# A two-layer decoder trunk on one Trainium2 core: stick-breaking attention with queries on partitions, its suffix sums by a VectorE scan and its probabilities turned through DRAM

## The chip, the cores and the metric

The kernel runs on one core of one Trainium2 chip. The metric is the device time of one execution in microseconds (us), the median of several runs. Times of single instructions, waits and transfers come from the hardware profiler's record of one execution. The engines are named as in the profile: PE (TensorE, the matmuls) with PEld (its weight loads), DVE (VectorE), ACT (ScalarE), POOL (GpSimd) and SP (SyncE, which issues most of the weight transfers). "ACTq" and "SPq" are the queues on which ACT and SP issue DMAs.

## The reference

A residual stream of 272 tokens (16 learned meta tokens and 256 of the sequence) by 2048 goes through two layers. Each layer is a token mixer with 16 heads of 128 and a squared-ReLU MLP of 8192. Layer 0 mixes with a softmax attention that has a forget gate. Layer 1 mixes with stick-breaking attention, whose K and V come from one projection `w_kv`; it is the part that the change touches:

```python
def stick_breaking_attention(q, k, v):
    for qs, qe in query_blocks(q.shape[1]):          # 16, then 128, then 128 queries
        z = einsum('bqhd,bkhd->bhqk', q[:, qs:qe], k[:, :qe]) * scale
        mask = k_pos[None, :] < q_pos[:, None]
        log_beta = log_sigmoid(z)
        log_one_minus = where(mask, log_sigmoid(-z), 0.0)
        suffix = cumsum(log_one_minus, axis=3, reverse=True) - log_one_minus
        a = where(mask, exp(log_beta + suffix), 0.0)
        outs.append(einsum('bhqk,bkhd->bqhd', a, v[:, :qe]))
```

With e = softplus(z), the logarithm of a probability is z minus the sum of e over this key and all later keys that the query sees. So a sum that runs backwards over the keys is wanted for each query and head. Only the 256 sequence tokens leave the kernel (after a last norm), so layer 1 has 256 queries and 272 keys.

## The kernel before

**The weight matmuls.** Activations lie with features on partitions and tokens on the free axis. All projections go through `gemm_group` (line 230): 512 output features, as four accumulators of 128 (`pacc`, four PSUM buffers), over four k blocks of 512 input features, 48 matmuls a block. Full f32 precision is had from split operands: each weight tile `raw` is copied by ACT to a rounded `whi` (line 225), and VectorE makes the rest, `wlo = raw - whi` (line 226); three matmuls (hi by hi, hi by lo, lo by hi) stand for one (line 192). A k block has two weight halves, so two `whi` and two `wlo`. `raw`, `whi` and `wlo` have four buffers each, that is two k blocks' worth. SP loads `raw` (line 214). Blocks 0 and 3 of a group go accumulator by accumulator and so need both halves at once; blocks 1 and 2 take the first half, then the second. The next group's accumulator m waits for the evacuation of this group's accumulator m by VectorE (`evac_kv`, line 472).

**Order.** The matmuls of PE are pinned one behind another in the order in which they are written (`gemm_matmul`, line 190); `placed_behind` and `behind` pin other instructions behind given matmuls. The list `issued` holds the matmuls of the running group, so `issued[140]` is its 141st. On each engine the rest is ordered by a scheduler at build time; each engine then runs its instructions in that order, and so does each engine's DMA queue: an instruction that waits holds back everything behind it, on ACT also the DMAs that ACT issues.

**Layer 0's attention (lines 462 to 609).** It has queries on partitions: `ps` of 144 and 272 keys, a softmax along the free axis, and then the probabilities must be turned, since the product with V sums over keys on partitions. They are turned in two steps: VectorE transposes 32 x 32 squares (line 543) into a tile `raw_p`, four DMAs write it to a scratch `p_dram` (line 546) and two DMAs read it back with the squares put in their places (line 567); then ACT and VectorE split the part that needs it.

**Layer 1's attention (lines 688 to 809).** A loop over four groups g of four heads. Each turn runs a K group of `w_kv`, the scores and probabilities, and a V group of `w_kv`; the products with V are the function `outputs1`, called ahead of k block 3 of the next turn's K group (line 690), and behind the last V group for g = 3. Then `out_proj` follows.

- Scores have keys on partitions: `pza` (128 keys by 256 queries, three matmuls of split operands) and `pzb` (the second 128 keys by the 144 queries that see them). The last 16 keys ("corner") are packed for four heads into one tile `kc` by POOL and have scores of their own, 64 columns.
- `softplus` (lines 693 to 698): three ACT passes and one on VectorE give e. Then e is split into `eh` (line 748) and `el` (line 749).
- The backward sums are matmuls with constant triangles: `ntri_r` (minus one at and above) and `nones_r` (all minus one), lines 756 to 761, six per pair of heads, into `pta` and `ptb`; `corner_sums` (lines 706 to 712) does the same for the corner.
- VectorE adds the sums to the scores (lines 765 to 768), ACT takes the exponential (line 773), and the part of the first 128 keys is split. The probabilities have keys on partitions already, as the product with V wants them.
- V is turned to token-major, for g below 3, by the same means as layer 0's probabilities: `squares` (line 401), `scratch` with eight writes to `v_dram` (line 412) and `values_back` with two reads (line 419), all on ACT's queue. For g = 3 PE turns it (`token_major`, line 389).

The tag "pp" names three SBUF slots of 1024 f32 a partition that are handed around between `e`, `eh`, `el`, `turned` and others; a new tile of a tag waits until the oldest of the three is done with.

## Time and profile before

| what | value |
| --- | --- |
| median of 3 runs | 2281.2 us (2281.03 to 2281.36) |
| span of the profiled execution | 2278.5 us |
| PE busy | 2271.1 us, 18898 matmuls |
| DVE busy | 1333.5 us |
| ACT busy | 1065.1 us |
| POOL busy | 39.4 us |
| HBM read and written | 413.85 MB and 8.41 MB |

The span is from the first to the last instruction of one execution; the run's time has some 2.7 us around it. "Busy" sums the time in which an engine executes, without the time in which it waits. A timeline row shows the start, the duration, the engine, the source line, the operation, the output and inputs, the shapes and how many instructions the row holds; in square brackets stands how long the engine had been idle before it and which instruction ended that. Matmuls are pipelined, so their durations overlap: what one costs a full PE is the distance between starts. A row that groups instructions by line gives the total and, behind the comma, the mean in ns.

### The profile page before, as it was taken

The page shows a single profiled execution, that of the slowest core. Times are in us where ns is not written, and L with a number is a line of the kernel's source. Part 1 is how long each engine was busy: PE and PEld are TensorE (multiplying, and loading weights), DVE is VectorE, ACT ScalarE, POOL GpSimd, SP SyncE. Part 2 cuts the span into 40 slices and gives each one's busy share as a digit, 9 for nine tenths or more (in the row PEclk, how much of TensorE's full clock was granted, in tenths as well). Part 3 has the DMA queues.
Part 4 walks back from the last instruction along what each step waited for, and adds up shares of the span by engine and source line. Part 5 has one row for each costly group of instructions (what it writes and reads, how often), then busy time and mean ns, then how long its engine had stood idle before and what let it go on. Part 6 is the DMA issues. An engine that isn't in the chain of part 4 may idle for free.

```text
span 2278.5 us, 44956 instructions
## 1 busy us (share of the span) xinstructions
PE 2271.1 (100%) x18898; PEld 2262.8 (99%) x18898; DVE 1333.5 (59%) x1930; ACT 1065.1 (47%) x1471; POOL 39.4 (2%) x72
## 2 busy tenths in 40 slices
PE   9999999999999999999999999999999999999998
PEld 9999999999999999999999999999999999999998
DVE  7767566554455455455566666666555555555555
ACT  6444445443354344335445555555443544543554
POOL 1000000000000000000000000000000000000001
PEclk9999999999999999999999999999999999999999
DMA  7765665555555555555556555555656556566564
GB/s 238 228 198 188 222 184 176 181 172 180 182 176 185 167 185 179 174 185 169 186 183 193 168 174 169 167 185 190 202 187 201 192 189 201 184 200 195 186 201 141
DMA packets 146171, 425.19 MB, mean 187 GB/s; under 512 B 31648, under 2 KB 43824, under 8 KB 145968
## 3 DMA queue, kind: packets, MB, share of 16 engines
q1 hardware_dynamic: 113760, 406.29, 54.1%
q10 hardware_dynamic: 32208, 16.02, 2.6%
q8 instruction: 148, 2.42, 0.4%
q14 instruction: 55, 0.45, 0.1%
HBM read 413.85 MB, written 8.41 MB: 185 GB/s over the span
## 4 chain that ended last, share of the span: by engine, by line
PE 99%; DMA 0%; issue 0%; POOL 0%; SPq 0%; POOLq 0%; ACT 0%; DVE 0%
PE acc L192 97%; PE po L435 0%; PE ps L435 0%; PE pza L435 0%; DMA raw<-w_qkv 0%; PE pzb L735 0%; PE po L804 0%; PE ps L508 0%; PE po L603 0%; PE pf L354 0%; PE pta L757 0%; PE pta L756 0%; PE pv L394 0%; POOL ob L850 0%; PE ptb L709 0%
## 5 line engine op out<-in xcount | busy, mean ns | idle before, releaser
L226 DVE TENSOR_TENSOR wlo<-raw,whi 128x1024 fp32r<-128x1024 f32 (+1 forms) x773 | 928.5, 1216 | 715.6 <-ACT whi L225 706.6
L225 ACT ACTIVATE whi<-raw 128x1024 fp32r<-128x1024 f32 (+1 forms) x773 | 796.4, 1050 | 961.0 <-PE acc L192 913.4
L192 PE MATMUL acc<-x_m,whi 128*128 128x272 f32 (+1 forms) x4096 | 643.1, 282 | 0.0
L192 PE MATMUL acc<-x_u,whi 128*128 128x272 f32 (+1 forms) x3968 | 626.0, 282 | 0.0
L192 PEld LDWEIGHTS acc<-x_m,whi 128*128 128x128 f32 x4096 | 566.0, 188 | 0.1
L192 PEld LDWEIGHTS acc<-x_u,whi 128*128 128x128 f32 x3968 | 550.4, 188 | 0.0
L192 PE MATMUL acc<-x_m,wlo 128*128 128x272 f32 (+1 forms) x2048 | 441.4, 282 | 0.0
L192 PE MATMUL acc<-x_u,wlo 128*128 128x272 f32 (+1 forms) x1984 | 432.1, 282 | 0.0
L192 PE MATMUL acc<-x_a,whi 128*128 128x272 f32 (+1 forms) x2048 | 355.4, 286 | 0.2 <-ACT whi L225 0.2
L192 PEld LDWEIGHTS acc<-x_m,wlo 128*128 128x128 f32 x2048 | 323.5, 188 | 0.0
L192 PEld LDWEIGHTS acc<-x_u,wlo 128*128 128x128 f32 x1984 | 315.3, 188 | 0.0
L192 PEld LDWEIGHTS acc<-x_a,whi 128*128 128x128 f32 x2048 | 301.3, 189 | 1.7 <-ACT whi L225 1.1
L192 PE MATMUL acc<-x_a,wlo 128*128 128x272 f32 (+1 forms) x1024 | 253.8, 286 | 0.0
L192 PE MATMUL acc<-x_kv,whi 128*128 128x272 f32 x1024 | 191.7, 288 | 0.0
L192 PEld LDWEIGHTS acc<-x_a,wlo 128*128 128x128 f32 x1024 | 175.7, 188 | 0.7 <-DVE ssq_a L158 0.4
L192 PE MATMUL acc<-x_o,whi 128*128 128x272 f32 (+1 forms) x1024 | 163.1, 283 | 0.0
L192 PEld LDWEIGHTS acc<-x_kv,whi 128*128 128x128 f32 x1024 | 160.1, 189 | 0.1
L192 PE MATMUL acc<-x_kv,wlo 128*128 128x272 f32 x512 | 147.6, 288 | 0.0
L192 PEld LDWEIGHTS acc<-x_o,whi 128*128 128x128 f32 x1024 | 142.3, 188 | 0.0
L307 DVE TENSOR_TENSOR hT<-acc,hT 128x272 f32<-128x272 f32 (+1 forms) x156 | 67.3, 431 | 75.4 <-PE acc L192 75.2
L192 PE MATMUL acc<-x_o,wlo 128*128 128x272 f32 (+1 forms) x512 | 110.7, 282 | 0.0
L192 PEld LDWEIGHTS acc<-x_kv,wlo 128*128 128x128 f32 x512 | 96.6, 189 | 0.0
(255 smaller groups left out, 1065.5 us busy)
## 6 DMA issues: line engine op xcount, KB each, us to landing
raw<-w_up SPq DMA_DIRECT2D x256, 512.0 KB, 3.9
raw<-w_dn SPq DMA_DIRECT2D x256, 512.0 KB, 4.0
raw<-w_qkv SPq DMA_DIRECT2D x92, 512.0 KB, 4.3
raw<-w_o SPq DMA_DIRECT2D x64, 512.0 KB, 3.9
raw<-w_kv SPq DMA_DIRECT2D x64, 512.0 KB, 4.4
raw<-w_q SPq DMA_DIRECT2D x32, 512.0 KB, 4.7
p_dram<-raw_p ACTq DMA_DIRECT2D x32, 96.0 KB, 4.6
v_dram<-turned ACTq DMA_DIRECT2D x48, 64.0 KB, 3.8
```

Of the source, the lines that this page charges most:

```text
L192: ins = nc.tensor.matmul(*args, **kw).ins
L225: on_act = nc.scalar.activation(hp, src, AF.Copy)
L226: on_dve = nc.vector.tensor_tensor(out=lp, in0=src, in1=hp.bitcast(F32), op=ALU.subtract)
L307: nc.vector.tensor_tensor(out=hT[:, c, t0:], in0=acc, in1=hT[:, c, t0:], op=ALU.add)
```

## The change

Layer 1's scores, probabilities and corner blocks are computed as in layer 0, with queries on partitions, and the triangular matmuls go.

- The constants `ntri`, `nones` and their copies and `maskC` go; `maskB` becomes 416 wide for the two query blocks (144 and 272 keys); `goes_on` is new, ones with a zero at the first place of each of the four runs of keys.
- The scores of a head: queries 128 to 255 by 272 keys with split operands (q2 against k, whose low half lies in a spare part of the output tile), queries 0 to 127 by 144 keys in f32. One VectorE add of the mask per head.
- `softplus` on 832 elements, then one `tensor_tensor_scan` of VectorE per pair of heads: state = state x goes_on + e, with e read backwards, so each run of keys starts anew. The scores minus the sums, read backwards, go through exp.
- `turn_probabilities` and `probabilities_back` are layer 0's turn through `p_dram`, made functions and used by both layers: six VectorE transposes, four DMA writes and two DMA reads per pair. In layer 1 the reads are pinned behind matmuls 140 and 176 of the V group, and the splits behind its last matmul.
- The corner probabilities are packed by POOL, transposed by PE (`pm`) and multiplied with `maskD`, as in layer 0, and the output tail is 128 columns wide.

```diff
+    def turn_probabilities(s, raw, pr):
+        y = raw[:, :768].rearrange("p (c h b i) -> p c h b i", c=4, h=2, b=3)
+        for i in range(2):
+            for b, o in enumerate((0, 144, 144 + P)):
+                nc.vector.transpose(y[:, :, i, b, :], s[:, 2 * pr + i, o:o + P].rearrange("p (c k) -> p c k", c=4))
+        y = y.rearrange("p c h b i -> p c (h b i)")
+        for a in range(4):
+            nc.scalar.dma_start(p_dram[pr].rearrange("c j a x -> a j c x")[a], y[32 * a:32 * a + 32])
+
+    def probabilities_back(pps, places):
+        for pr, at in enumerate(places):
+            raw, p0, p1 = pps[pr]
+            back = p_dram[pr].rearrange("c j a (h x) -> (c j) (a h) x", h=2)
+            for dst, src in ((raw[:, :512], back[:, :, :64]), (p1.rearrange("p i q -> p (i q)"), back[:, :, 64:])):
+                behind(nc.scalar.dma_start(dst.rearrange("p (m x) -> p m x", m=8), src), issued[at])
...
+        k0 = att.tile([P, 4, T], F32R, tag="vT", bufs=1, name=f"k0_{g}")
+        k1 = ao.spare[:, 4 * g:4 * g + 4]
+        for j in range(0, 4, 2):
+            nc.scalar.activation(k0[:, j:j + 2], kT[:, j:j + 2], AF.Copy)
+            nc.vector.tensor_tensor(out=k1[:, j:j + 2], in0=kT[:, j:j + 2], in1=k0[:, j:j + 2].bitcast(F32),
+                                    op=ALU.subtract)
+        q2 = att.tile([P, 2, 4, P], F32R, tag="pp", bufs=3, name=f"q12_{g}")
+        split(q2, q[:, :, P:S])
...
         for pr in range(2):
-            nc.tensor.matmul(pa, ntri_r, e_hi[:, :, 0:256], start=True, stop=False)
-            nc.tensor.matmul(pa, ntri_r, e_lo[:, :, 0:256], start=False, stop=False)
-            nc.tensor.matmul(pa[:, :, 112:], nones_r, e_hi[:, :, 256:400], start=False, stop=False)
-            nc.tensor.matmul(pa[:, :, 112:], nones_r, e_lo[:, :, 256:400], start=False, stop=True)
-            nc.tensor.matmul(pb[:, :, :144], ntri_r, e_hi[:, :, 256:400], start=True, stop=False)
-            product = nc.tensor.matmul(pb[:, :, :144], ntri_r, e_lo[:, :, 256:400], start=False, stop=True)
...
+            zp = z[:, 2 * pr:2 * pr + 2]
             for i in range(2):
+                product = by_parts(ps[:, 144:416], [q2[:, k, j, :] for k in range(2)], [k0[:, j], k1[:, j]], True, True)
+                placed_behind(nc.tensor.matmul(ps[:, 0:144], q[:, j, 0:P], kT[:, j, :144], start=True, stop=True), product)
+                nc.vector.tensor_tensor(out=z[:, j], in0=ps[:, :416], in1=maskB, op=ALU.add)
+            softplus(e.rearrange("p (i k) -> p i k", i=2), zp)
+            nc.vector.tensor_tensor_scan(out=sums, data0=goes_on.rearrange("p i k -> p (i k)"), data1=backward(e), initial=0.0,
+                                         op0=ALU.mult, op1=ALU.add)
+            nc.vector.tensor_tensor(out=zf, in0=zf, in1=backward(sums), op=ALU.subtract)
+            nc.scalar.activation(zp, zp, AF.Exp)
+            raw = att.tile([P, 2, 2, 256], F32, tag="pp", bufs=3, name=f"raw_p1_{g}_{pr}").rearrange("p x i q -> p (x i q)")
...
+            turn_probabilities(z, raw, pr)
+            pps.append((raw, p0, p1))
...
         gemm_group(w_kv[2 * g + 1], xc, 0, lambda m, acc: evac_kv(m, acc, vT))
+        probabilities_back(pps, (140, 176))
+        for pr in range(2):
+            raw, p0, p1 = pps[pr]
+            behind(split(p0.rearrange("p x i q -> p x (i q)"), raw[:, :512]), issued[-1])
```

In the order that each engine gets at build time, SP's list of instructions is the same before and after; ACT's queue has 22 transfers instead of 10 in each of the groups 0 to 2.

More of the change, by code (lines that the diff above doesn't have):

```diff
@@ L63, in yoco_kernel @@
     make_identity(nc, ident)
-    nones = const.tile([P, P], F32, name="nones")
-    nc.vector.memset(nones, -1.0)
-    nones_r = const.tile([P, P], F32R, name="nones_r")
-    nc.vector.tensor_copy(nones_r, nones)
-    ntri = const.tile([P, P], F32, name="ntri")
-    nc.gpsimd.memset(ntri, -1.0)
-    nc.gpsimd.affine_select(out=ntri, in_=ntri, compare_op=ALU.is_ge, fill=0.0, base=0,
-                            pattern=[[-1, P]], channel_multiplier=1)
-    ntri_r = const.tile([P, P], F32R, name="ntri_r")
-    nc.vector.tensor_copy(ntri_r, ntri)
     maskA = const.tile([P, 416], F32, name="maskA")
@@ L89, in yoco_kernel @@
                             pattern=[[32, 4], [0, 32]], channel_multiplier=-1)
-    maskB = const.tile([P, 400], F32, name="maskB")
+    maskB = const.tile([P, 416], F32, name="maskB")
     nc.gpsimd.memset(maskB, 0.0)
-    nc.gpsimd.affine_select(out=maskB[:, 0:256], in_=maskB[:, 0:256], compare_op=ALU.is_gt, fill=-BIG,
-                            base=M, pattern=[[1, 256]], channel_multiplier=-1)
-    nc.gpsimd.affine_select(out=maskB[:, 256:400], in_=maskB[:, 256:400], compare_op=ALU.is_gt, fill=-BIG,
-                            base=0, pattern=[[1, 144]], channel_multiplier=-1)
-    maskC = const.tile([P, 4, M], F32, name="maskC")
-    nc.gpsimd.memset(maskC, 0.0)
-    nc.gpsimd.affine_select(out=maskC, in_=maskC, compare_op=ALU.is_gt, fill=-BIG, base=M,
-                            pattern=[[32, 4], [1, M]], channel_multiplier=-1)
-    nc.gpsimd.affine_select(out=maskC, in_=maskC, compare_op=ALU.is_ge, fill=-BIG, base=-M,
-                            pattern=[[-32, 4], [0, M]], channel_multiplier=1)
+    nc.gpsimd.affine_select(out=maskB[:, 0:144], in_=maskB[:, 0:144], compare_op=ALU.is_gt, fill=-BIG,
+                            base=M, pattern=[[-1, 144]], channel_multiplier=1)
+    nc.gpsimd.affine_select(out=maskB[:, 144:416], in_=maskB[:, 144:416], compare_op=ALU.is_gt, fill=-BIG,
+                            base=M + P, pattern=[[-1, T]], channel_multiplier=1)
+    goes_on = const.tile([P, 2, 416], F32, name="goes_on")
+    nc.gpsimd.memset(goes_on, 1.0)
+    for t in (0, T):
+        nc.gpsimd.memset(goes_on[:, :, t:t + 1], 0.0)
     maskD = const.tile([P, 8, M], F32, name="maskD")
@@ L132, in __init__ @@
             if t0:
-                self.wide = rows[:, :, :n + 6]
+                self.wide, self.spare = rows[:, :, :n + 6], rows[:, :, d:d + T]
                 nc.gpsimd.tensor_copy(rows[:, :, n:n + 6], pad[:, :6].unsqueeze(1).to_broadcast([P, NC, 6]))
@@ L459, in put_split, with in_order @@
         nc.vector.tensor_tensor(out=lo, in0=src, in1=hi.bitcast(F32), op=ALU.subtract)
+    def turn_probabilities(s, raw, pr):
[12 more added lines that the diff above has]
+                behind(nc.scalar.dma_start(dst.rearrange("p (m x) -> p m x", m=8), src), issued[at])
+    def in_order(p0, p1):
+        p0 = p0.rearrange("p x i q -> p x (i q)").rearrange("p x (a h b i) -> p x h b a i", a=4, h=2, b=2)
+        p0 = [[p0[:, k, i] for i in range(2)] for k in range(2)]
+        return p0, p1.rearrange("p i q -> p (i q)").rearrange("p (a h i) -> p h a i", a=4, h=2)
     ao = Split("o0", 0)
@@ L538, in yoco_kernel @@
             p1 = tmp.tile([P, T], F32, tag="relu", name=f"p1_{g}_{pr}")[:, :2 * P].rearrange("p (i q) -> p i q", i=2)
-            y = raw[:, :768].rearrange("p (c h b i) -> p c h b i", c=4, h=2, b=3)
-            for i in range(2):
-                for b, o in enumerate((0, 144, 144 + P)):
-                    nc.vector.transpose(y[:, :, i, b, :], s[:, 2 * pr + i, o:o + P].rearrange("p (c k) -> p c k", c=4))
-            y = y.rearrange("p c h b i -> p c (h b i)")
-            for a in range(4):
-                nc.scalar.dma_start(p_dram[pr].rearrange("c j a x -> a j c x")[a], y[32 * a:32 * a + 32])
+            turn_probabilities(s, raw, pr)
             pps.append((raw, p0, p1))
@@ L560, in yoco_kernel @@
         gemm_group(w_qkv0[3 * g + 2], xa, 0, lambda m, acc: evac_kv(m, acc, vT))
-        for pr, at in enumerate((140, 176 if g else 191)):
-            raw, p0, p1 = pps[pr]
-            back = p_dram[pr].rearrange("c j a (h x) -> (c j) (a h) x", h=2)
-            for dst, src in ((raw[:, :512], back[:, :, :64]), (p1.rearrange("p i q -> p (i q)"), back[:, :, 64:])):
-                behind(nc.scalar.dma_start(dst.rearrange("p (m x) -> p m x", m=8), src), issued[at])
+        probabilities_back(pps, (140, 176 if g else 191))
         pv = patt.tile([P, 512], F32, tag="patt", name=f"pvm_{g}")
@@ L594, in outputs @@
                 raw, p0, p1 = pps[pr]
-                p0 = p0.rearrange("p x i q -> p x (i q)").rearrange("p x (a h b i) -> p x h b a i", a=4, h=2, b=2)
-                p0 = [[p0[:, k, i] for i in range(2)] for k in range(2)]
-                p1 = p1.rearrange("p i q -> p (i q)").rearrange("p (a h i) -> p h a i", a=4, h=2)
+                p0, p1 = in_order(p0, p1)
                 v0, v1 = vs[pr] if turned is not None else token_major(vT, pr, 0, f"0_{g}_{pr}")
@@ L685, in yoco_kernel, with backward, softplus @@
                    after={kb: (lambda kb=kb: split_c(kb)) for kb in range(4)} if g else {})
+    def backward(a):
+        (step, n), = a.ap[1:]
+        return bass.AP(a.tensor, a.offset + (n - 1) * step, [a.ap[0], (-step, n)])
+    def softplus(e, z):
+        nc.scalar.activation(e, z, AF.Abs)
+        nc.scalar.activation(e, e, AF.Exp, scale=-1.0)
+        nc.scalar.activation(e, e, AF.Ln, bias=1.0)
+        nc.vector.scalar_tensor_tensor(out=e, in0=z, scalar=0.0, in1=e, op0=ALU.max, op1=ALU.add)
     ao = Split("o1", M)
@@ L691, in yoco_kernel @@
         q = qT1[g]
-        def softplus(e, z):
-            nc.scalar.activation(e, z, AF.Abs)
-            nc.scalar.activation(e, e, AF.Exp, scale=-1.0)
-            nc.scalar.activation(e, e, AF.Ln, bias=1.0)
-            nc.vector.scalar_tensor_tensor(out=e, in0=z, scalar=0.0, in1=e, op0=ALU.max, op1=ALU.add)
-        kc = packed(kT[:, :, 240:T], f"kc_{g}")
-        zc = att.tile([P, 64], F32, tag="s0", name=f"zc_{g}")
-        ec = att.tile([P, 64], F32, tag="ec", name=f"ec_{g}")
-        sc = att.tile([P, 4, M], F32, tag="sc", name=f"sc_{g}")
@@ L706, in corner_sums @@
-        def corner_sums(pt, product, zc=zc, ec=ec, sc=sc):
-            for i, left in enumerate((ntri, nones)):
-                placed_behind(nc.tensor.matmul(pt[:, i, :], left, ec, start=True, stop=True), product)
-            nc.vector.tensor_tensor(out=zc, in0=pt[:, 0, :], in1=zc, op=ALU.add)
-            nc.scalar.activation(zc, zc, AF.Exp)
-            nc.vector.tensor_copy(sc, pt[:, 1, :].rearrange("p (h q) -> p h q", h=4))
-        def pp_tile(dtype, name):
-            t = att.tile([P, 2, 2, 256], dtype, tag="pp", bufs=3, name=name)
-            return t.rearrange("p a i q -> p (a i q)")[:, :832].rearrange("p (i q) -> p i q", i=2)[:, :, :400]
@@ L720, in yoco_kernel @@
-        k0 = att.tile([P, 4, T], F32R, tag="vT", bufs=1, name=f"k0_{g}")
-        k0 = k0.rearrange("p h t -> p (h t)")[:, :1024].rearrange("p (a h t) -> p a h t", a=2, h=4)
-        split(k0, kT[:, :, 0:P])
-        put_split(ao, 4 * g, 4, M, S, q[:, :, :S])
+        k0 = att.tile([P, 4, T], F32R, tag="vT", bufs=1, name=f"k0_{g}")
+        k1 = ao.spare[:, 4 * g:4 * g + 4]
[3 more added lines that the diff above has]
+                                    op=ALU.subtract)
@@ L724, in yoco_kernel @@
+        q2 = att.tile([P, 2, 4, P], F32R, tag="pp", bufs=3, name=f"q12_{g}")
+        split(q2, q[:, :, P:S])
         z = att.tile([P, 4, 416], F32, tag="s", bufs=1, name=f"z_{g}")
+        pps = []
         for pr in range(2):
-            zp = z[:, 2 * pr:2 * pr + 2, :400]
-            pa = patt.tile([P, 2, 256], F32, tag="patt", name=f"pza_{g}_{pr}")
-            pb = patt.tile([P, 2, 256], F32, tag="patt", name=f"pzb_{g}_{pr}")
+            zp = z[:, 2 * pr:2 * pr + 2]
             for i in range(2):
@@ L730, in yoco_kernel @@
                 j = 2 * pr + i
-                product = by_parts(pa[:, i, :], [k0[:, k, j, :] for k in range(2)],
-                                   [x[:, 4 * g + j] for x in (ao.hi, ao.lo)], True, True)
-            for i in range(2):
-                j = 2 * pr + i
-                placed_behind(nc.tensor.matmul(pb[:, i, :144], kT[:, j, P:2 * P], q[:, j, 112:S], start=True, stop=True), product)
-            if pr == 0:
-                pz = pb[:, 0, 192:]
-                placed_behind(nc.tensor.matmul(pz, kc, q[:, :, 240:S], start=True, stop=True), product)
@@ L740, in yoco_kernel @@
-            nc.vector.tensor_tensor(out=zp[:, :, 0:256], in0=pa, op=ALU.add,
-                                    in1=maskB[:, 0:256].unsqueeze(1).to_broadcast([P, 2, 256]))
-            nc.vector.tensor_tensor(out=zp[:, :, 256:400], in0=pb[:, :, :144], op=ALU.add,
-                                    in1=maskB[:, 256:400].unsqueeze(1).to_broadcast([P, 2, 144]))
-            e = pp_tile(F32, f"e_{g}_{pr}")
-            e_hi = pp_tile(F32R, f"eh_{g}_{pr}")
-            e_lo = pp_tile(F32R, f"el_{g}_{pr}")
@@ L747, in yoco_kernel @@
-            softplus(e, zp)
-            nc.scalar.activation(e_hi, e, AF.Copy)
-            nc.vector.tensor_tensor(out=e_lo, in0=e, in1=e_hi.bitcast(F32), op=ALU.subtract)
-            if pr == 0:
-                nc.vector.tensor_tensor(out=zc, in0=pz, in1=maskC.rearrange("p h q -> p (h q)"), op=ALU.add)
-                softplus(ec, zc)
-            pa = patt.tile([P, 2, 256], F32, tag="patt", name=f"pta_{g}_{pr}")
-            pb = patt.tile([P, 2, 256], F32, tag="patt", name=f"ptb_{g}_{pr}")
@@ L762, in yoco_kernel @@
-            if pr == 0:
-                corner_sums(pb[:, :, 192:], product)
-            for t in (240, 384):
-                nc.vector.tensor_tensor(out=zp[:, :, t:t + M], in0=zp[:, :, t:t + M],
-                                        in1=sc[:, 2 * pr:2 * pr + 2, :], op=ALU.add)
-            nc.vector.tensor_tensor(out=zp[:, :, 0:256], in0=pa, in1=zp[:, :, 0:256], op=ALU.add)
-            nc.vector.tensor_tensor(out=zp[:, :, 256:400], in0=pb[:, :, :144], in1=zp[:, :, 256:400], op=ALU.add)
@@ L770, in yoco_kernel @@
-        ps = []
-        for pr in range(2):
-            zp = z[:, 2 * pr:2 * pr + 2, :400]
+                ps = patt.tile([P, 512], F32, tag="patt", name=f"pz_{g}_{j}")
+                product = by_parts(ps[:, 144:416], [q2[:, k, j, :] for k in range(2)], [k0[:, j], k1[:, j]], True, True)
+                placed_behind(nc.tensor.matmul(ps[:, 0:144], q[:, j, 0:P], kT[:, j, :144], start=True, stop=True), product)
+                nc.vector.tensor_tensor(out=z[:, j], in0=ps[:, :416], in1=maskB, op=ALU.add)
@@ new lines, in yoco_kernel @@
+            e, sums = (att.tile([P, 2, 2, 256], F32, tag="pp", bufs=3, name=f"{x}_{g}_{pr}")
+                       .rearrange("p x i q -> p (x i q)")[:, :832] for x in ("e", "sums"))
+            softplus(e.rearrange("p (i k) -> p i k", i=2), zp)
+            nc.vector.tensor_tensor_scan(out=sums, data0=goes_on.rearrange("p i k -> p (i k)"), data1=backward(e), initial=0.0,
+                                         op0=ALU.mult, op1=ALU.add)
+            zf = zp.rearrange("p i k -> p (i k)")
+            nc.vector.tensor_tensor(out=zf, in0=zf, in1=backward(sums), op=ALU.subtract)
@@ L773, in yoco_kernel @@
             nc.scalar.activation(zp, zp, AF.Exp)
+            raw = att.tile([P, 2, 2, 256], F32, tag="pp", bufs=3, name=f"raw_p1_{g}_{pr}").rearrange("p x i q -> p (x i q)")
             p0 = att.tile([P, 4, T], F32R, tag=("kT", "qT")[pr], bufs=(1, 4)[pr], name=f"p01_{g}_{pr}")
-            p0 = p0.rearrange("p h t -> p (h t)")[:, :1024].rearrange("p (a i q) -> p a i q", a=2, i=2)
-            split(p0, zp[:, :, 0:256])
-            ps.append(p0)
+            p0 = p0.rearrange("p h t -> p (h t)")[:, :1024].rearrange("p (x i q) -> p x i q", x=2, i=2)
@@ new lines, in yoco_kernel @@
+            p1 = tmp.tile([P, T], F32, tag="relu", name=f"p11_{g}_{pr}")[:, :2 * P].rearrange("p (i q) -> p i q", i=2)
+            turn_probabilities(z, raw, pr)
+            pps.append((raw, p0, p1))
+        pm = patt.tile([P, 512], F32, tag="patt", name=f"pm1_{g}")
+        placed_behind(nc.tensor.transpose(pm[:, 0:P], corners(z[:, :, P:144], z[:, :, 400:416], f"sm1_{g}"), ident), product)
+        pm_sb = att.tile([P, 192], F32, tag="pm_sb", bufs=1, name=f"pm_sb1_{g}")
+        nc.vector.tensor_tensor(out=pm_sb[:, :P].rearrange("p (b q) -> p b q", q=M), in1=maskD, op=ALU.mult,
+                                in0=pm[:, P - M:P].unsqueeze(1).to_broadcast([P, 8, M]))
@@ L785, in yoco_kernel, with outputs1 @@
             scratch(turned, issued[-2:])
-        def outputs1(g=g, vT=vT, z=z, zc=zc, ps=ps, turned=turned):
+        def outputs1(g=g, vT=vT, pps=pps, pm_sb=pm_sb, turned=turned):
             if turned is not None:
@@ L790, in outputs1 @@
             pv = patt.tile([P, 512], F32, tag="patt", name=f"pvc_{g}")
-            nc.tensor.transpose(pv[:, :P], packed(vT[:, :, 240:T], f"vc_{g}"), ident)
+            nc.tensor.transpose(pv[:, :P], corners(vT[:, :, P:144], vT[:, :, 256:T], f"vc1_{g}"), ident)
             vc_sb = att.tile([P, P], F32, tag="vm_sb", bufs=1, name=f"vc_sb_{g}")
             nc.scalar.copy(vc_sb, pv[:, :P])
-            own = att.tile([P, 8, M], F32, tag="own", bufs=1, name=f"own1_{g}")[:, :4]
+            own = att.tile([P, 8, M], F32, tag="own", bufs=1, name=f"own1_{g}")
             for pr in range(2):
@@ L797, in outputs1 @@
                 po = patt.tile([P, 2, 256], F32, tag="patt", name=f"po1_{g}_{pr}")
+                p0, p1 = in_order(*pps[pr][1:])
                 for i in range(2):
-                    j = 2 * pr + i
-                    product = weighted(po, v0, [[ps[pr][:, k, h, :] for h in range(2)] for k in range(2)], i)
-                    if j == 0:
-                        placed_behind(nc.tensor.matmul(pv[:, P:P + 64], vc_sb, zc, start=True, stop=True), product)
-                        nc.scalar.copy(own, pv[:, P:P + 64].rearrange("p (h q) -> p h q", h=4))
-                    nc.tensor.matmul(po[:, i, 112:], v1[:, i, :], z[:, j, 256:400], start=False, stop=i == 1)
-                nc.vector.tensor_tensor(out=po[:, :, 240:], in0=po[:, :, 240:], in1=own[:, 2 * pr:2 * pr + 2], op=ALU.add)
+                    product = weighted(po, v0, p0, i)
+                    if pr == i == 0:
+                        placed_behind(nc.tensor.matmul(pv[:, P:2 * P], vc_sb, pm_sb[:, :P], start=True, stop=True), product)
+                        nc.scalar.copy(own, pv[:, P:2 * P].rearrange("p (c q) -> p c q", c=8))
+                    nc.tensor.matmul(po[:, i, P:], v1[:, i, :], p1[:, i], start=False, stop=i == 1)
+                ends = po.rearrange("p i (c q) -> p (i c) q", c=2)[:, :, P - M:]
+                nc.vector.tensor_tensor(out=ends, in0=ends, in1=own[:, 4 * pr:4 * pr + 4], op=ALU.add)
                 put_split(ao, 4 * g + 2 * pr, 2, M, S, po)
```

## The prediction

> **What bounds the kernel now.** I read the page's busy table first, then the chain of work that ended last, then the costliest groups.

> ```profile
> span 2278.5 us, 44956 instructions
> ...
> PE 2271.1 (100%) x18898; PEld 2262.8 (99%) x18898; DVE 1333.5 (59%) x1930; ACT 1065.1 (47%) x1471; POOL 39.4 (2%) x72
> ...
> PE 99%; DMA 0%; issue 0%; POOL 0%; SPq 0%; POOLq 0%; ACT 0%; DVE 0%
> ...
> L226 DVE TENSOR_TENSOR wlo<-raw,whi 128x1024 fp32r<-128x1024 f32 (+1 forms) x773 | 928.5, 1216 | 715.6 <-ACT whi L225 706.6
> L225 ACT ACTIVATE whi<-raw 128x1024 fp32r<-128x1024 f32 (+1 forms) x773 | 796.4, 1050 | 961.0 <-PE acc L192 913.4
> ```

> PE never stops: 2271.1 of 2278.5 us, and 99% of the chain. So a matmul taken away is worth its full time, and any wait that reaches PE costs its full length. The last two rows name what feeds PE: every weight tile goes through a split on ACT (whi, 1.05 us), then one on VectorE (wlo, 1.22 us). ACT sits idle 913 us until PE frees a buffer: the splits run as far ahead as their four buffers each allow, which is two k blocks of a group, and no further. The span is one execution's; the median, 2281.2, is 2.7 us more. I work with differences and put them on the median.

> **What PE is spared.** The timeline of PE, with starts on the left; between two starts lies what the work costs a full PE. The first two rows are layer 0, which already has queries on partitions; the rest is layer 1.

> ```profile
> 212.63 0.41 PE L508 MATMUL ps<-kT,qT 128*128 128x144 f32 x2
> ...
> 213.25 0.41 PE L508 MATMUL ps<-kT,qT 128*128 128x144 f32 x2
> ...
> 1302.87 0.39 PE L756 MATMUL pta<-eh,ntri_r 128*128 128x512 f32 x1
> ...
> 1303.23 0.88 PE L435 MATMUL pza<-x_o,k 128*128 128x256 f32 x6
> 1303.94 0.41 PE L735 MATMUL pzb<-qT,kT 128*128 128x144 f32 x2
> 1304.09 0.49 PE L757 MATMUL pta<-el,ntri_r 128*128 128x512 f32 x1
> ...
> 1304.82 0.33 PE L709 MATMUL ptb<-ec,ntri 128*128 128x64 f32 x2
> ...
> 1305.21 0.46 PE L735 MATMUL pzb<-qT,kT 128*128 128x144 f32 x2
> ...
> 1330.07 0.29 PE L192 MATMUL acc<-x_kv,wlo 128*128 128x272 f32 x1
> ...
> 1330.44 0.28 PE L192 MATMUL acc<-x_kv,wlo 128*128 128x272 f32 x1
> ```

> Removed in each head group g (there are four, of two pairs of heads): the triangular sums, 0.36 + 0.73 = 1.09 us a pair (1302.87 to 1303.23, 1304.09 to 1304.82), so 2.18; the corner sums, 0.39 (to 1305.21); the corner's own scores, 0.15 by the pzb row beside them. The scores change form: two heads took 0.71 (1303.23 to 1303.94) and 0.15 for each head's pzb, 0.50 a head; the new form is layer 0's, 0.62 a head (212.63 to 213.25), so +0.48 for four. The corner probabilities now need one transpose, another 0.15 or so. The output products keep their number; their tails get a little narrower and the corner's wider, which I leave out. Net 2.18 + 0.39 + 0.15 - 0.48 - 0.15 = 2.1 us a group, 8.4 in all. If nothing ever waits: 2281.2 - 8.4 = 2272.8.

> A weight matmul costs 0.123 us (three from 1330.07 to 1330.44), a k block of 48 of them 5.9, a group of four 23.7. I set t = 0 at the start of a V group. With 2.5 us of scores in it, V ends at 26.1; the next K group's blocks start at 26.1, 32.0, 37.9 and 43.8, and the group's outputs stand at the head of the last of these.

> **VectorE and ACT.** The scan is not in layer 1 of before; its nearest row is layer 0's, on 272 elements of 16 partitions, 2.6 ns an element.

> ```profile
> L372 DVE TENSOR_TENSOR_SCAN fc<-fx,fe x1: 711/711/711, 49.0 to 49.0; 16x272 f32<-16x272 f32 x1
> ```

> ```profile
> L472 DVE TENSOR_TENSOR vT<-acc,rstd_a 128x272 f32<-128x272 f32 x16 | 6.9, 434 | 1.4 <-PE acc L192 1.4
> L386 DVE TENSOR_TENSOR p<-z,p 128x512 fp32r<-128x512 f32 x8 | 5.5, 688 | 7.0 <-ACT p L385 7.0
> ```

> ```profile
> L773 ACT ACTIVATE z<-z 128x800 f32<-128x800 f32 x8 | 6.9, 863 | 13.8 <-DVE z L768 13.8
> ```

> ```profile
> L543 DVE STREAM_TRANSPOSE raw_p<-s 128x128 f32<-128x128 f32 x24 | 5.9, 284 | 0.0
> ```

> By elements the 832-wide scan is at most 832 x 2.61 = 2.2 us; with the fixed part that the next two rows leave (272 and 512 elements: 1.06 ns an element, 0.15 us fixed) it is 0.15 + 832 x 2.06 = 1.9 us, which I take. [...] The subtraction that reads the sums backwards I take at 1.0 us (832 x 1.06 + 0.15); nothing of before reads backwards, so twice that is its upper bound. Exp is 0.9, six transposes a pair 6 x 0.284 = 1.7. What leaves VectorE is the subtraction e_lo, the adds from two PSUM tiles and the splits of the probabilities as they stood. VectorE is 59% busy over the span, so its totals do not decide; the order does.

> **What is added that can wait.** The probabilities are turned through DRAM: per pair four writes and two reads, all issued on ACT's own queue, which executes in order. The read of a pair waits there until its four writes have landed, and the ACT split of the pair waits for the read. In the order of the changed build, behind pair 1's split stand in groups 0 and 2 the second whi of k block 2 and all of block 3 of the next K group, in group 1 those of block 3 alone. The same waits have a row of their size in layer 0 and in the values' turn:

> ```profile
> p_dram<-raw_p ACTq DMA_DIRECT2D x32, 96.0 KB, 4.6
> ...
> raw_p<-p_dram ACTq DMA_DIRECT2D x8, 256.0 KB, 6.5
> ```

> ```profile
> L546 ACTq DMA_DIRECT2D p_dram<-raw_p x32: 309/444/821, 74.3 to 304.7; - x32
> ...
> DMA to landing us min/median/max: 1.8/4.9/8.3
> ```

> ```profile
> 1432.58 1.11 ACTq L421 DMA_DIRECT2D turned<-v_dram  x2
> 1433.73 1.06 ACT L225 ACTIVATE whi<-raw 128x1024 fp32r<-128x1024 f32 x1 [0.96 <-DMA v_dram<-turned]
> 1435.17 0.42 ACT L385 ACTIVATE v<-turned 128x256 fp32r<-128x256 f32 x1 [0.38 <-DMA turned<-v_dram]
> ```

> Columns of the first view: issuer, count, size, median us from issue to landing. Of the second: an issue's own ns, then the landings. The third shows ACT: a weight split that waits for a write's landing, and values used 2.6 us after their read was issued (1432.58 to 1435.17). So the write lies between 1.8 and 4.6 us, the read between 2.6 and 6.5: together 4.4 to 11.1. I take 8.0, near the middle: 3.7 and 4.3.

> [...]

> **Site A, pair 0.** Its reads are pinned to matmuls late in the V group and are issued at 22.9 (g0, g2) or 23.5 (g1, g3). Landing 27.2 or 27.8; ACT split 0.6 (863 x 512/800); VectorE split 0.7, 28.5 or 29.1; behind it VectorE evacuates V's third accumulator, 0.43. PE wants that bank for the third quarter of K's block 0, at 26.1 + 3.0 = 29.1. Stall 0 or 0.4; a subtraction stands before the fourth evacuation and adds some 0.3. I take 0.3 and 0.7: 2.0 in four groups.

> **Site B, pair 1.** Its exp stands on ACT behind pair 0's split and two weight splits, and behind VectorE's subtraction: done at 31.1. VectorE has two wlo to make first; the transposes run 33.0 to 34.5. The four writes issue 0.44 apart as squares come ready, the last at 35.5; landed 39.2; read landed 43.5; split 44.1. Then whi 45.2 and wlo 46.4. PE wants them in groups 0 and 2 for the second half of block 2, at 37.9 + 3.0 = 40.9: stall 5.5. In group 1 it wants the first weights of block 3 at 43.8: 2.6. In group 3 the output projection follows with 256 columns and its products wait for the split near the end of its third block, behind the first pair's, at 42.7 by the same counting; 44.1 and 0.7 on VectorE come 2.1 late. Sum 5.5 + 2.6 + 5.5 + 2.1 = 15.7.

> **Site C, the values.** Their eight writes and two reads stand behind the same block, at the outputs PE waits for their splits again: once PE resumes it needs 3 to 6 us to reach them, while a read with its splits takes 4.3 + 0.4 + 0.4. I take 1.7, 1.3 and 1.7 for groups 0 to 2 and nothing in group 3, which turns its values on PE: 4.7.

> Sum: 2.0 + 15.7 + 4.7 = 22.4. 2272.8 + 22.4 = 2295, **slower by 0.6%**. The range of this case alone is 2285 to 2305, for 6.2 to 9.5 us of write and read.

> **The rivals.** Of no change one can tell here only what is over 0.2%, 4.6 us: below 2276.6 is faster, above 2285.8 slower.

> First, the landings are quick (1.8 and 2.6). Site B shrinks by 3.6, and by 0.5 more if the writes issue at their least, 0.31 us: 1.4 + 0 + 1.4 + 0; A and C shrink to nothing. 2272.8 + 2.8 = 2275.6, faster. The values' 2.6 us speaks for it, the medians of the very transfers that are copied here speak against. It decides when write and read stay under 4.5 us. [...] Chance 0.19.

> Second, the halves cancel: write and read at 5.5 to 6, B at 3 + 0 + 3 + 0, C and A at 2 together, 2281. The shorter case of layer 0 (the minimum 1.8 with a 4 us read) speaks for it. Chance 0.14.

> Third, long: 4.6 and 6.5. B grows by 3.1 each to 28.1, A by 2.2 each to 10.8, C stays: 2272.8 + 43.6 = 2316. The medians speak for it; against it, layer 0 runs the same transfers beside a PE that the page shows without gaps. A backward read at twice its price adds 1.0 a pair to the same chain and lands here too. Chance 0.17.

> That the change costs the path nothing at all, because two k blocks of weights (11.8 us) are split ahead, is the first rival at its best: 2272.8.

> **How the numbers follow.** Forecast 0.50, rivals 0.19, 0.14, 0.17. Faster takes the first, less a little for those of its cases that end within the bound, 0.18; same takes the second and that remainder, 0.15; slower the forecast and the third, 0.67. The range runs from 2274, just under the first rival, to 2317, the third.

> **What would show it.** Right: PE idle in layer 1 in seven or so gaps, the longest of 3 to 6 us in the third k block of the K group, released by wlo, with whi behind a landing of p_dram; the PE busy sum down by about 8 us; scans near 1.9 us each. Wrong: PE still without gaps (first rival), or gaps at the scan or at evacuations, released by VectorE and not by a DMA (VectorE is the bound). A write and read of under 5 us together would turn the sign.

## The result, and the profile after

The changed kernel takes 2304.95 us (median of 4 runs, 2299.98 to 2306.89) against 2281.28 us before (4 runs): a ratio of 1.0101, 95% interval 1.0087 to 1.0116. It is slower by 23.7 us, 1.0%; the forecast was 2295 us. The profiled execution is the quickest of the four, 2299.98 us.

The page after, with the rows that answer to those shown of before:

```profile
span 2298.2 us, 44896 instructions
...
PE 2270.4 (99%) x18830; PEld 2259.3 (98%) x18830; DVE 1343.1 (58%) x1943; ACT 1057.8 (46%) x1451; POOL 37.9 (2%) x78
...
PE 92%; DMA 3%; DVE 2%; issue 1%; ACTq 1%; ACT 1%; POOL 0%; SPq 0%; POOLq 0%; DVEq 0%
```

PE has 68 matmuls fewer and is still busy for 2270.4 us, 0.7 less than before. The chain that ended last, which was PE's for 99% of the span, now runs through DMAs, VectorE and ACT for 7% of it. In the changed kernel L177 is the weight matmul, L210 and L211 make whi and wlo, L480 evacuates V, L370 and L371 split the probabilities, and L454 and L461 issue the writes to `p_dram` and the reads back. Where PE waited is told by the view of waits, for PE alone (who waited, for whom; us in total, times, the longest):

```profile
PE acc L177 <- ACT whi L210: 9.1, 4, 3.2
PE acc L177 <- DVE vT L480: 4.9, 4, 1.7
PE po L420 <- ACT p L370: 2.4, 1, 2.4
PE pm L737 <- POOL pk_sm L438: 2.1, 4, 1.1
PE acc L177 <- DVE wlo L211: 1.9, 3, 0.7
...
PE po L420 <- DVE p L371: 0.2, 1, 0.2
```

One of the four waits for whi, 0.2 us, lies in layer 0 and is there in the kernel before too. The others, 20.3 us, lie in layer 1, where PE waited for nothing before. The waits for whi and wlo, and group 3's for the probabilities, are the forecast's site B: 8.8 + 1.9 + 2.4 + 0.2 = 13.3. Those for vT are site A, 4.9. The wait of the corner's transpose, 2.1, was in no sum.

ACT's timeline in group 0 shows how they come about; "ACTq" rows are DMAs that it issues, and in brackets stands how long ACT had been idle and what ended that:

```profile
1300.92 1.89 ACTq L454 DMA_DIRECT2D p_dram<-raw_p  x4
...
1307.49 0.54 ACTq L461 DMA_DIRECT2D raw_p<-p_dram  x1
1308.06 0.89 ACTq L461 DMA_DIRECT2D p<-p_dram  x1
1313.27 0.63 ACT L370 ACTIVATE p<-raw_p 128x512 fp32r<-128x512 f32 x1 [6.83 <-DMA raw_p<-p_dram]
...
1319.78 2.05 ACTq L454 DMA_DIRECT2D p_dram<-raw_p  x4
1321.88 1.65 ACTq L401 DMA_DIRECT2D v_dram<-turned  x3
1324.78 0.53 ACTq L461 DMA_DIRECT2D raw_p<-p_dram  x1
...
1329.38 0.63 ACT L370 ACTIVATE p<-raw_p 128x512 fp32r<-128x512 f32 x1 [10.82 <-DMA raw_p<-p_dram]
...
1330.28 1.06 ACT L210 ACTIVATE whi<-raw 128x1024 fp32r<-128x1024 f32 x1 [0.27 <-ACT p L370]
```

Pair 0: the fourth write is issued by 1302.81, its read at 1307.49, and its split begins at 1313.27. So the read waits 4.7 us for the writes, and the split 5.8 for the read. Pair 1: 1321.83, 1324.78, 1329.38, that is 3.0 and 4.6. ACT executes nothing for 6.8 us at the first place and 10.8 at the second (it issues DMAs there), and the weight split that PE wants begins only at 1330.28.

Pair 1's split in groups 1 and 2:

```profile
1393.40 0.63 ACT L370 ACTIVATE p<-raw_p 128x512 fp32r<-128x512 f32 x1 [12.39 <-DMA v_dram<-turned]
...
1451.26 0.63 ACT L370 ACTIVATE p<-raw_p 128x512 fp32r<-128x512 f32 x1 [9.90 <-DMA v_dram<-turned]
```

There the profile names a write of the values, issued behind the reads on the same queue, as what ended the wait. So in these two groups it is not shown that a landing of `p_dram` came last.

The rest of the loss is no wait. Windows of the same stretch (us of the window, then busy us and number of each engine, then PE's granted clock, the DMA share and GB/s):

```profile
1328.00:1332.00 4.00, 0.68 (x4) 0.30 (x2) 1.32 (x2) 2.35 (x3) 0.00 (x0) 1.00 0.73 138
1332.00:1336.00 4.00, 3.35 (x15) 3.35 (x16) 4.00 (x5) 3.56 (x8) 0.00 (x0) 0.61 0.91 269
1336.00:1340.00 4.00, 4.00 (x34) 4.00 (x33) 1.90 (x4) 1.06 (x1) 0.00 (x0) 0.96 0.95 362
```

Behind the gap the clock is granted at 0.61 over 4 us, and 15 matmuls run there, against 34 in the next 4 us (PE still waits for the first 0.65 us of the 4). The same in the chain, at the three places of site B in groups 0 to 2 (start, us, what):

```profile
1332.65 5.53 PE acc L177 x30
...
1396.29 6.18 PE acc L177 x30
...
1454.63 5.54 PE acc L177 x30
```

Thirty matmuls cost 3.7 us at the full clock (0.123 each); these take 17.25 in place of 11.1, so the lowered clock costs 6.2 us at these three places. In before the whole stretch from 1261 to 1500 is granted 1.00.

### The profile page after: what moved, and what is told of

Its sections match the earlier page's. It is cut to its first block, busy times and chain, and to the rows that moved or that the text cites. A ratio compares the mean times of both kernels' runs of the same rounds, so it can differ in the third digit from the quotient of the medians.

```text
span 2298.2 us, 44896 instructions
## 1 busy us (share of the span) xinstructions
PE 2270.4 (99%) x18830; PEld 2259.3 (98%) x18830; DVE 1343.1 (58%) x1943; ACT 1057.8 (46%) x1451; POOL 37.9 (2%) x78
## 4 chain that ended last, share of the span: by engine, by line
PE 92%; DMA 3%; DVE 2%; issue 1%; ACTq 1%; ACT 1%; POOL 0%; SPq 0%; POOLq 0%; DVEq 0%
PE acc L177 90%; DMA p_dram<-raw_p 1%; DMA raw_p<-p_dram 1%; DVE wlo L211 1%; PE po L420 0%; ACT whi L210 0%; ACTq L454 0%; DMA p<-p_dram 0%; DVE sums L723 0%; DVE z L726 0%; PE ps L420 0%; PE pz L420 0%; DMA v_dram<-turned 0%; DVE raw_p L451 0%; ACTq L461 0%
## 5 line engine op out<-in xcount | busy, mean ns | idle before, releaser
L211 DVE TENSOR_TENSOR wlo<-raw,whi 128x1024 fp32r<-128x1024 f32 (+1 forms) x773 | 927.3, 1216 | 694.6 <-ACT whi L210 687.7
L210 ACT ACTIVATE whi<-raw 128x1024 fp32r<-128x1024 f32 (+1 forms) x773 | 796.0, 1050 | 941.1 <-PE acc L177 895.0
L177 PE MATMUL acc<-x_m,whi 128*128 128x272 f32 (+1 forms) x4096 | 643.0, 281 | 0.0
L177 PE MATMUL acc<-x_u,whi 128*128 128x272 f32 (+1 forms) x3968 | 626.0, 281 | 0.0
L177 PEld LDWEIGHTS acc<-x_m,whi 128*128 128x128 f32 x4096 | 565.8, 188 | 0.1
L177 PEld LDWEIGHTS acc<-x_u,whi 128*128 128x128 f32 x3968 | 550.3, 188 | 0.0
L177 PE MATMUL acc<-x_m,wlo 128*128 128x272 f32 (+1 forms) x2048 | 440.7, 281 | 0.0
L177 PE MATMUL acc<-x_u,wlo 128*128 128x272 f32 (+1 forms) x1984 | 431.5, 281 | 0.0
L177 PE MATMUL acc<-x_a,whi 128*128 128x272 f32 (+1 forms) x2048 | 354.9, 286 | 0.2 <-ACT whi L210 0.2
L177 PEld LDWEIGHTS acc<-x_m,wlo 128*128 128x128 f32 x2048 | 323.3, 188 | 0.0
L177 PEld LDWEIGHTS acc<-x_u,wlo 128*128 128x128 f32 x1984 | 315.1, 188 | 0.0
L177 PEld LDWEIGHTS acc<-x_a,whi 128*128 128x128 f32 x2048 | 300.8, 188 | 1.5 <-ACT whi L210 0.5
L177 PE MATMUL acc<-x_a,wlo 128*128 128x272 f32 (+1 forms) x1024 | 253.5, 285 | 0.0
L177 PE MATMUL acc<-x_kv,whi 128*128 128x272 f32 x1024 | 199.0, 293 | 12.3 <-ACT whi L210 8.8
L177 PEld LDWEIGHTS acc<-x_kv,whi 128*128 128x128 f32 x1024 | 164.6, 193 | 13.7 <-ACT whi L210 9.5
L177 PEld LDWEIGHTS acc<-x_a,wlo 128*128 128x128 f32 x1024 | 175.5, 188 | 0.8 <-DVE ssq_a L143 0.4
L177 PE MATMUL acc<-x_o,whi 128*128 128x272 f32 (+1 forms) x1024 | 163.0, 282 | 1.4 <-DVE vT L480 1.4
L177 PE MATMUL acc<-x_kv,wlo 128*128 128x272 f32 x512 | 150.0, 293 | 1.9 <-DVE wlo L211 1.9
L177 PEld LDWEIGHTS acc<-x_o,whi 128*128 128x128 f32 x1024 | 142.2, 188 | 1.6 <-DVE vT L480 1.6
L177 PE MATMUL acc<-x_o,wlo 128*128 128x272 f32 (+1 forms) x512 | 110.8, 282 | 0.0
L177 PEld LDWEIGHTS acc<-x_kv,wlo 128*128 128x128 f32 x512 | 99.1, 194 | 2.7 <-DVE wlo L211 2.7
## 6 DMA issues: line engine op xcount, KB each, us to landing
raw_p<-p_dram ACTq DMA_DIRECT2D x16, 256.0 KB, 5.4
```

Of the source, the lines that this page charges most:

```text
L177: ins = nc.tensor.matmul(*args, **kw).ins
L210: on_act = nc.scalar.activation(hp, src, AF.Copy)
L211: on_dve = nc.vector.tensor_tensor(out=lp, in0=src, in1=hp.bitcast(F32), op=ALU.subtract)
```

## The experiments

Each is an edit of the changed kernel. Ratios are against the kernel before, in runs on the same chip.

**Without the DRAM turn.** Layer 1 issues no writes to `p_dram` and no reads; the split takes the transposed squares as they lie, and POOL fills `p1` with zeros.

```diff
-        probabilities_back(pps, (140, 176))
...
-            turn_probabilities(z, raw, pr)
+            turn_probabilities(z, raw, pr, False)   # transposes only
+            nc.gpsimd.memset(p1, 0.0)
```

> The changed kernel without the DRAM turn in layer 1: no writes to p_dram and no reads; the split takes the transposed squares as they lie, and the probabilities of the second 128 keys are zeros that POOL writes. Scan, subtraction and the six transposes a pair stay. Theory Q (the waits for p_dram's landings on ACT's in-order queue hold back the weight splits): PE's gaps at the K groups' start and in their third block go, and with them the lowered clock; what stays is the saving of the V groups, 6.8 us, against some 2.3 us at the corner's transpose: about 2277 us (2274 to 2280). Rival V (VectorE's scan, subtraction and transposes are what comes late): all of these stay, so the gaps stay, and the time stays above 2295.

Measured 2274.3 us, ratio 0.997 (0.9958 to 0.9982). The page of this kernel:

```profile
span 2271.5 us, 44836 instructions
...
PE 2262.7 (100%) x18830; PEld 2254.1 (99%) x18830; DVE 1344.2 (59%) x1943; ACT 1059.3 (47%) x1451; POOL 38.3 (2%) x86
```

All gaps at A, B and the corner are gone (1.5 us of waits for the values, site C, are left), though VectorE's work is the same (DVE 1344.2 us): rival V, VectorE as the bound by itself, falls. The run also closes the account of the profiled executions. The same 18830 matmuls keep PE busy for 2262.7 us here, 8.4 less than before, and for 2270.4 in the changed kernel. So the change of form spares PE 8.4 us, matmuls that run slower take 7.7 of them back, and the waits add 20.3: -8.4 + 7.7 + 20.3 = 19.6, where the spans differ by 2298.2 - 2278.5 = 19.7. Of the 7.7, the lowered clock is seen to take the 6.2 above; the rest was not traced.

**Pair 1's reads and split later.**

```diff
-        probabilities_back(pps, (140, 176))
+        probabilities_back(pps, ((0, 140),))            # groups 0 to 2
...
         def outputs1(...):                              # ahead of the next K group's block 3
+                probabilities_back(pps, ((1, 100),))
+                probability_split(1, 136)
```

> Only the place of pair 1's two reads and of its split moves, in groups 0 to 2: pinned behind the 101st and the 137th matmul of the next K group instead of the 177th and the last of the V group. Q: the gaps of 3 to 4 us in the third or fourth block of the K group go, and the lowered clock behind them (about 1.7 us each); the gaps at the K groups' start, at the corner's transpose and all of group 3 stay: 16 us off the changed kernel, about 2289 us (2284 to 2293). V: the same VectorE work in the same places, so no change, 2300 to 2307.

Measured 2289.8 us (2287.91 to 2290.86), 1.0037 (1.0023 to 1.0052). PE's waits in this kernel:

```profile
PE pm L737 <- POOL pk_sm L438: 4.2, 4, 1.3
PE acc L177 <- DVE vT L480: 3.2, 2, 1.6
...
PE acc L177 <- DVE wlo L211: 1.0, 2, 0.7
...
PE acc L177 <- ACT whi L210: 0.3, 1, 0.3
```

This is the forecast time. The waits for whi and wlo in layer 1 fall from 10.7 to 1.3 us, while PE, VectorE and ACT execute as many instructions as in the changed kernel. What stood behind the turn's waits on ACT's queue was the cost of site B. One thing does not fit: PE's clock is seen lowered only once here, in group 3 (0.50 from 1488 to 1490), and its busy sum is still 2269.4 us, 6.7 above the kernel without the DRAM turn. So the busy sum holds more than the clock.

**Keeping PE busy in the gaps.** Small matmuls of 128 columns, their result unread, in PE's order at the three places; 12 each, then 16 each with the second place corrected.

```diff
+    def filler(n, u):
+        t = patt.tile([P, 512], F32, tag="patt", name=f"idle_{u}")
+        for _ in range(n):
+            ins = nc.tensor.matmul(t[:, :P], mean_w, mean_w, start=True, stop=True).ins
```

> The changed kernel with 12 matmuls of 128 columns, whose result nobody reads, in PE's order at the three places where it stands idle for 3 to 4 us (groups 0 to 2), some 2.8 us of work in each. The waits stay as they are. Theory C (PE's granted clock falls to 0.6 for some 4 us because PE stood idle): the clock stays at 1.00 there, 1.7 us saved at each place, 5 us in all, about 2300 us (2297 to 2302). Rival (the lowered clock has another cause, or costs nothing): 2304 to 2308.

> As e4_warm, with 16 matmuls (some 3.8 us) ahead of the second half of the third block of the K group in all three places: in e4_warm they stood behind the gap in one place, and the wait outlasted them in another. C: the gaps there shrink below 1.5 us, the clock stays at 1.00, and the 30 matmuls behind each place take 3.7 us and not 5.5 to 6.2; 4 to 6 us off the changed kernel, 2299 to 2302, unless the landings are slower in this run. Rival (the clock has another cause): the 30 matmuls still take 5.5 us, 2304 to 2308.

Measured 2309.8 us (1.0127; 1.0111 to 1.0142) and 2306.9 us (1.0119; 1.0104 to 1.0134): no gain, against both expectations; the totals lie at or above what the rivals gave. The windows behind the three places in the second of them:

```profile
1334.00:1337.00 3.00, 3.00 (x25) 2.98 (x25) 3.00 (x3) 2.11 (x4) 0.00 (x0) 1.00 0.80 224
1398.00:1402.00 4.00, 3.25 (x27) 3.11 (x26) 4.00 (x4) 3.64 (x7) 0.00 (x0) 1.00 0.80 242
1460.00:1464.00 4.00, 3.26 (x19) 3.24 (x19) 4.00 (x4) 3.61 (x7) 0.00 (x0) 0.72 0.83 250
```

and one of its waits of PE:

```profile
PE po L430 <- ACT v L380: 3.3, 1, 3.3
```

The clock part holds in part: filled, two of the three places keep a clock of 1.00, which all three had lost. The third falls to 0.72, and in group 3, which was not filled, the clock now falls behind a wait of 1.99 us (0.54 from 1506 to 1508). The total doesn't follow. In group 0 PE reaches the outputs sooner and then waits 3.3 us for the values, which come through DRAM on the same queue and for which the changed kernel does not wait. In groups 1 and 2 the idle matmuls (3.73 us) and the waits left behind them come to 6.0 and 6.2 us, where the changed kernel waits 3.2 and 3.6; why the weights are no earlier there was not traced. So what the clock takes can't be taken off by itself. Behind how much idle time the clock falls isn't settled either: behind idle pieces of 1.56 and 0.75 us (second place) it stayed at 1.00, behind 1.75 and 0.74 (third) it was 0.72.

**Everything late.** On top of pair 1's, pair 0's split goes behind the K group's first matmuls and the corner's transpose into the next K group; a second kernel also has PE turn group 3.

```diff
-            behind(split(...), issued[-1])              # pair 0
+        gemm_group(..., {1: lambda: probability_split(0, 36), 3: outputs1})
...
+            behind(nc.tensor.transpose(pm[:, 0:P], pk_sm, ident), issued[60])
```

> e2_pair1_late, and in groups 0 to 2 pair 0's split pinned behind the 37th matmul of the next K group (so that V's last evacuations and the K group's weight splits stand ahead of it), and in all groups the corner's transpose moved behind the 61st matmul of the next K group (in group 3 behind the V group). Q: no gap is left in groups 0 to 2; group 3 keeps some 3.8 us: 2273 + 4 to 5 = 2277 to 2279. V: VectorE has the same work, gaps of 1 to 2 us a group stay: 2285.

> e5_all_late, and in group 3, which has no K group behind it to hide in, the turn by PE as in e6_pe_turn: two pairs at some 0.6 us on PE and no gap. Q: 2273 + 1 to 2 = 2274 to 2276, the best of all. If the landings of groups 0 to 2 reach the outputs, 2279 or more.

Measured 2288.1 us (1.0033; 1.0021 to 1.0045) and 2281.9 us (1.0006; 0.9997 to 1.0016): both miss the time given first. The first lies past even the 2285 of V, but its waits are for weight splits in groups 0 to 2 and, in group 3, for vT (2.1 us) and for the values that PE turns there (3.0 us). ACT's timeline of the second, in group 2:

```profile
1428.54 2.82 ACTq L454 DMA_DIRECT2D p_dram<-raw_p  x4
1431.45 4.02 ACTq L401 DMA_DIRECT2D v_dram<-turned  x8
1435.58 1.06 ACT L210 ACTIVATE whi<-raw 128x1024 fp32r<-128x1024 f32 x1 [9.46 <-DMA v_dram<-turned]
```

and its windows in group 0:

```profile
1322.00:1326.00 4.00, 2.62 (x20) 2.17 (x18) 1.31 (x2) 2.11 (x3) 0.00 (x0) 1.00 0.55 136
1326.00:1330.00 4.00, 3.74 (x17) 3.75 (x18) 4.00 (x5) 3.68 (x8) 0.00 (x0) 0.57 0.99 256
```

In the second kernel site A and the corner are free of gaps, but the new order puts twelve writes ahead of the first weight split of block 2. They take 6.8 us to issue (2.82 + 4.02). The forecast of these runs had counted the waits for landings and not the issues. No run takes the issues alone away, so this cause is read from the timeline and not tested. And the clock falls behind idle pieces of only 0.89 and 0.75 us, to 0.57 from 1326 to 1330.

**The turn on PE.** Six transposes of 128 x 128 a pair on PE, split straight from PSUM; no squares and no `p_dram` in layer 1.

```diff
-            turn_probabilities(z, raw, pr)
+            for i in range(2):
+                for b, o in enumerate((0, 144)):
+                    nc.tensor.transpose(pa[:, i, b, :], z[:, 2 * pr + i, o:o + P], ident)
+                nc.tensor.transpose(pb[:, i, :], z[:, 2 * pr + i, 144 + P:144 + 2 * P], ident)
+            split(p0, pa)
+            nc.scalar.copy(p1, pb)
```

> The probabilities are turned by PE (six transposes of 128 x 128 a pair) and split straight from PSUM; no VectorE squares, no p_dram in layer 1. Q: no wait of ACT for a landing is left but the values'; PE pays 8 pairs x 6 transposes x 0.11 to 0.15 us = 5 to 7 us: about 2283 us (2280 to 2286). V: the scan and the subtraction stay, so gaps stay: above 2290.

> e6_pe_turn once more, with more rounds, beside e10_mixed: 2278 to 2279, 0.1% below the kernel before.

Measured 2278.8 us (0.9990; 0.9981 to 0.9999), and again 2278.6 us (0.9992; 0.9983 to 1.0001). No gap is left in layer 1, and the clock is 1.00 in every window read there; the scan and the subtraction are the changed kernel's. It comes out 4 us better than expected; the corner's wait, 2.1 us in the changed kernel, is gone as well, and the rest of the 4 was not traced.

**The scan twice**, in the kernel with the turn on PE:

```diff
+            for _ in range(2):
                 nc.vector.tensor_tensor_scan(out=sums, ...)
```

> e6_pe_turn with every scan made twice, 8 x 1.9 = 15 us more on VectorE. If the scan hides beside PE, as the forecast took it: 2279, at most 2281. If VectorE's chain sets the pace once the DMA waits are gone: up to 2294.

Measured 2276.8 us (0.9984; 0.9974 to 0.9993), not longer than with one scan. Its scans:

```profile
L724 DVE TENSOR_TENSOR_SCAN sums<-goes_on,e 128x832 f32<-128x832 f32 x16 | 30.1, 1883 | 0.0
```

15 us more on VectorE cost nothing: once no DMA stands in the way, the scan is hidden. That says nothing of the changed kernel, where it is not (see the account below).

**One pair each way**: pair 0 through DRAM with its split late, pair 1 by PE; then group 3 wholly by PE.

```diff
+            if pr == 0:                                  # second kernel: and g < 3
                 turn_probabilities(z, raw, pr)
...
+        gemm_group(..., {1: lambda: turn(40), 3: outputs1})
```

> Pair 0 through p_dram as in the changed kernel, with its split behind the 41st matmul of the next K group; pair 1 by PE's transposes at the same place. If pair 0's landings are hidden where nothing but two weight splits stands behind them, PE saves one of two turns a group against e6_pe_turn, 0.3 to 0.45 us each: 2277 to 2278. If they are not, gaps at the K groups' start come back: 2280 or more.

> e10_mixed with both pairs of group 3 turned by PE, since no K group follows in which pair 0's landing could hide: in e10_mixed's profile PE waited 2.8 us there and its clock was lowered behind it (3.4 us by windows of 2 us). One more turn on PE costs 0.63 us. If that gap is what is left: 2276.4 - 2.8 - 1.5 to 3 + 0.6 = 2271.5 to 2273 in a run with it, 2273 to 2275 in the median; if group 3's gap was that one profile's own, no change, 2276 to 2277.

Measured 2276.4 us (0.9982; 0.9973 to 0.9990) and 2276.5 us (0.9983; 0.9974 to 0.9992). The first beats both kernels, by 4 us and by 28. It is also 2.2 us faster than the turn on PE alone, measured beside it on the same chip (2276.41 against 2278.57): a trip through DRAM behind which little stands costs less than six transposes. The second gains nothing over the first, which fits a gap of that one execution, the slowest of its eleven (2278.85 us).

## Why the prediction was right, and where its sizes were off

- **PE is the bound, and 8.4 us of matmuls go.** Right: 2271.1 - 2262.7 = 8.4, read in the kernel without the DRAM turn.
- **VectorE.** The rows after, grouped by line: scan 1.88 us for a forecast of 1.9, subtraction 1.02 for 1.0 (so the backward reading costs nothing here; the upper bound of twice that was the author's estimate, with no row behind it), so the sizes are right. The doubled scan shows that there is room for them where PE does the turn.

```profile
L723 DVE TENSOR_TENSOR_SCAN sums<-goes_on,e 128x832 f32<-128x832 f32 x8 | 15.1, 1883 | 0.0
...
L726 DVE TENSOR_TENSOR z<-z,sums 128x832 f32<-128x832 f32 x8 | 8.1, 1017 | 0.0
```

  In the changed kernel itself both stand in the chain that ended last, ahead of the turn. In group 0 (start, us, what):

```profile
1294.63 1.88 DVE sums L723
...
1297.55 1.03 DVE z L726
...
1302.24 5.18 DMA p_dram<-raw_p
...
1307.49 5.76 DMA raw_p<-p_dram
...
1313.27 0.64 ACT p L370
```

  So they are hidden only while nothing as long as the turn stands behind them. What a shorter scan would gain in the changed kernel was not run.

- **The mechanism: weight splits stand behind landings on ACT's queue.** Right, and shown by moving two reads and a split (10.7 to 1.3 us of waits) and by taking the DMAs out. Of the signs given, the gaps and their place came true; they were ended more by whi (8.8 us) than by wlo (1.9), the longest was 3.2 us, and PE's busy sum fell by 0.7 us and not by about 8, since slower matmuls took 7.7 back.
- **Site B, 15.7 us.** Measured 13.3, at the places that were named: the second half of block 2 in groups 0 and 2, block 3 in group 1, the outputs of group 3. By group it is 4.0, 3.2, 3.6 and 2.6 us, where 5.5, 2.6, 5.5 and 2.1 were forecast. From the last write to pair 1's split went 7.6 us in groups 0 and 2 and 10.2 in group 1, where 8.0 was taken for write and read.
- **Site A, 2.0 us.** Too small: 4.9. Pair 0's write and read took 4.7 + 5.8 = 10.5 us in group 0. The forecast's sum for this site goes by the read alone: it took 4.4 to 6.2 us in the four groups, where 4.3 was taken for both pairs.
- **Site C, 4.7 us.** None in the changed kernel. It turns up (3.3 us) where PE is kept at its clock.
- **Not in the sum:** the slower matmuls, 7.7 us, of which 6.2 are seen at a lowered clock, and the wait of the corner's transpose, 2.1. A gap was priced at its own length; what follows it at a lowered clock was left out. This is the step that kept 2295 below the measured time. The waits together came to 20.3 us for a forecast of 22.4, and that they came so near is in part luck: A was 2.9 too small and the corner's 2.1 put at nothing, while B was 2.4 and C 4.7 too large. In group 0, against a clock of 1.00, the 0.61 over 4 us and the 0.96 over the next 4 come to 1.7 us (0.39 x 4 + 0.04 x 4), near the 1.8 by which the thirty matmuls there take longer (5.53 for 3.7).

By these sizes the sum is -8.4 + 7.7 + 4.9 + 13.3 + 2.1 = 19.6 in the profiled execution. The three other runs are 5 to 7 us longer; what grew in them was not seen, so this part of the 23.7 us stays open.

The first rival (write and read under 4.5 us together) fell with 7.6 and 10.5. The second, at 5.5 to 6, fell with it. The third, 4.6 and 6.5 us, is near what pair 0 took (4.7 and 5.8), but its time of 2316 was not reached.

## What to carry to other kernels

On a queue that runs in order, cost an added DMA by what stands behind its wait and behind its issue, and read the built order for that: here two reads and a split, moved by two to three k blocks, were worth 15 us. Where a matmul engine has no gap, price each new gap with the slow matmuls that can follow it, not by its length alone: here a lowered clock took 6.2 us behind gaps of 10.8 (site B in groups 0 to 2). And a round trip through DRAM that spares the matmul engine work can cost more than the work: with both pairs, six transposes a pair on PE were 26 us cheaper than the trip as first placed. With one pair, and little behind its waits, the trip was the cheaper by 2 us.
